# Two transformer-like blocks on one core: gate groups, projection and modulation moved; opening, border and end rewritten

## The chip, the cores and the metric

The kernel runs on one core of a Trainium2 chip. Five engines share the work: PE (TensorE, matrix products into PSUM banks), DVE (VectorE), ACT (ScalarE), POOL (GpSimd, nearly unused here) and SP (SyncE, which here only issues DMAs). Each engine takes its instructions in one fixed order. The metric is the time of one execution in microseconds of device time, lower is better.

## What is computed

The input has 512 tokens of width 2048. A first block (a gated convolution and a gated recurrence, their gated sum, and an embedding gate), a second block (dilated attention and two-way retention, modulated by a vector c) and a last norm follow one another. Cut to what matters:

```
def first_block(x, p, ...):
    h = rmsnorm(x, norm_mix_g)
    c_g, b_g, xa, za, q, fl, iv, og, ga, gb = split(h @ w_in)      # 4 x 1024, 4 x 1024, 2 x 2048
    ya = b_g * causal_dwconv3(c_g * xa, conv_w) * silu(za)
    o  = hgrn2_chunked(silu(q), kk(fl, lb), iv, log_f(fl, lb))     # 8 heads of 128
    yb = rmsnorm_per_head(o) * hg_norm_g * silu(og)
    m  = sigmoid(ga) * (ya @ w_a_out) + sigmoid(gb) * (yb @ w_b_out)
    x  = x + m @ w_o
    gate = sigmoid(rmsnorm(x, ple_norm_g) @ w_ple_gate)
    x  = x + gate * (p @ w_ple_proj)                               # p is 512 x 256
    return rmsnorm(x, final_norm_g)

def second_block(x, c, ...):
    shift, scale, gate = split(silu(c) @ w_ada + b_ada)            # w_ada is 2048 x 6144
    h = rms_norm(x, g) * (1 + scale) + shift
    q_a, k_a, v_a, z_a, q_r, k_r, v_r, z_r = split(h @ w_in)
    y = concat(dilated_attention_mixture(q_a, k_a, v_a) * silu(z_a),
               bidirectional_retention(q_r, k_r, v_r) * silu(z_r))
    x = x + gate * (y @ w_out)
    return rms_norm(x, final_gain)
```

## The kernel before, in words

**Products.** Activations stand in SBUF with features on partitions and the 512 tokens along the row, each as a rounded f32r part and a rest. Weights come from memory in chunks of 128x1024 f32 (512 KB). ACT makes the rounded part whi of a chunk (L245), DVE the rest wlo (L256). Each 128x128 weight tile then takes three matmuls of 128x512 (L355 to L357, in `mm3`): a chunk is 24 matmuls. Where the tokens are to be on partitions (`group_wide`), the three are L497 to L499. Ten gate groups go through a fast algorithm with 128x256 matmuls (L412 to L414). A group (`group_fm`) is 2 output tiles of 128 features: two PSUM banks of the pool ps_mm and 96 matmuls, when it has four chunks.

**PSUM.** There are eight banks: four of ps_mm for the large products, two of ps_sd and two of ps_so for side work. A product that needs a bank waits until the tile last in it has been read.

**What sets the order.** The program is written out by a Python planner: `chunk()` and `group_fm()` write the large products in a fixed plan (`plan_w`, `plan_wide`, `plan_dual`), and after each few matmuls call `tick()` (L156), which takes one step of a generator in each of the queues side, side2, post and slow. So the small work (norms, recurrence, modulation) is mixed into the products at those steps, and its place on DVE, ACT and PE is fixed when the program is written. `drain(cond)` (L171) takes steps until a condition holds.

**Stages in order**, with the time at which their first product starts in the trace: opening and norm of x with the first groups of w_in (0 us), the wide values w_v (57 us), the recurrence pairs pr = 1, 2, 3 with their groups fl, q and og (from 103 us), the plain gate groups i = 10 to 15 of w_in (up to 594 us), ten fast groups, w_a and w_b (1140 us), w_o (1314 us), w_gate (1488 us), the border to the second block with `dual("w_in2", ...)` (1664 us), w_v2 (1713 us), attention and retention, w_out (2375 us), whose last part is done in two halves of 256 tokens (from 2505 us), and the output.

**The places of the change.** `start_gen` (L702) squares the tokens' features, adds them (L715), makes row sums on PE (L574: the 128x128 squares are the weights and a column of ones the moving side), then sqrt (L720), reciprocal (L721), a diagonal matrix (L584) and a product with ones (L581, `spread`) that gives the norm factor R0 on all partitions (L726). Then it scales the features for later use (L739) and splits them (L545). The gate branch's first products are not yet normed and are scaled by R0 on the way out of PSUM (`times`, L984). `lower_bound` (L688) is a chain of small DVE instructions. `rec_gen` is the recurrence, whose last steps for pair 3 (exponentials L792 on ACT, products L895 and L898 on PE) run into the gate groups. `p_gen` and `ple_proj` (L1118) compute p @ w_ple_proj, one 128x1024 chunk for each of 4 groups: four ps_mm banks, 6 matmuls each, copied out by ACT (L1129) and DVE (L1131) and stored to memory. `ada_gen` (L1046) computes silu(c) @ w_ada row by row on DVE (L1068): each of 192 steps loads 256 KB. `h2_gen` (L1442) makes both norms at the border: two sums over partitions by products with ones (L561, L562, 128x512), a chain of 128x512 instructions and a reciprocal (L1457), then the features of the second block (L1466, L1467, L537, L543). `half_tail` and `finish` (L1849) close each half: row sums (L574), sqrt (L1854), reciprocal (L1855), diagonal (L584), spread (L581), a scaling of each of eight 128x512 pieces (L1864) and a DMA for each (L1865).

## Time and profile before

| what | value |
|---|---|
| time, median of 3 runs | 2569.77 us (2568.53 to 2569.97) |
| the profiled execution's own time | 2568.21 us |
| its span, first to last instruction | 2566.3 us |
| PE busy | 2535.8 us (99%) |
| DVE busy | 1724.2 us (67%) |
| ACT busy | 1023.8 us (40%) |
| mean granted TensorE clock | 0.994 of full speed |
| moved by DMA | 372 MB, mean 145 GB/s |

The span is what one execution's trace covers, and the time has some two microseconds more around it. PE is busy for nearly the whole span, so the table says only that the time is PE's work. A change that leaves the products alone can gain only what PE waits or runs slowly, and that is found place by place: in the windows (busy time and clock of a stretch), in the list of waits, and in the timeline of the stretch. A row of the trace such as "466.84 0.80 PE L355 ... [4.14 <-ACT s L1174]" reads: the instruction of line 355 started at 466.84 us and took 0.80 us, PE had stood idle for 4.14 us, and what ended the wait was ACT's instruction of line 1174. Matmuls overlap, so the distance of two starts, and not the duration, is what one costs.

### The profile page before, as it was taken

To read this page: it belongs to the slowest core of one execution; us is meant where nothing else is said; L and a number is where in the kernel's file an instruction comes from. 1 tells how busy PE (TensorE), PEld (TensorE's weight loads), DVE (VectorE), ACT (ScalarE), POOL (GpSimd) and SP (SyncE) were. 2 spreads that over 40 slices of the span, in tenths; PEclk is the share of its full clock that TensorE was granted. 3 is DMA by queue.
4 is the path that set the end of the run, shared out by engine and by line. 5 is a ranking of instruction groups with operands and counts; after the bars stand their busy time and mean duration, and the time that the engine had idled before them with its cause. 6 is when DMAs were issued, how large, how long until landed. Compare 5 with 4: busy or idle time off the path is not lost.

```text
span 2566.3 us, 34681 instructions
## 1 busy us (share of the span) xinstructions
PE 2535.8 (99%) x13796; PEld 2202.4 (86%) x13796; DVE 1724.2 (67%) x2938; ACT 1023.8 (40%) x1345; POOL 1.3 (0%) x9
## 2 busy tenths in 40 slices
PE   9999999899999999999999999999999999999998
PEld 7888888788999999998888888878888888888888
DVE  6768578787888988886656665576535446774445
ACT  6545255343344444443222344364323334442333
POOL 0000000000000000000000000000000000000000
PEclk9999999999999999999999999999999999999999
DMA  5322322474333334467656665352222325384345
GB/s 194 90 58 92 97 83 86 145 249 160 105 110 116 116 95 145 132 214 266 225 188 244 222 213 168 126 191 74 92 92 79 112 75 192 129 279 142 120 131 156
DMA packets 140595, 372.45 MB, mean 145 GB/s; under 512 B 15377, under 2 KB 20113, under 8 KB 140433
## 3 DMA queue, kind: packets, MB, share of 16 engines
q1 hardware_dynamic: 137680, 367.65, 43.9%
q10 hardware_dynamic: 2752, 2.58, 0.3%
q8 instruction: 108, 1.77, 0.3%
q14 instruction: 55, 0.44, 0.1%
HBM read 336.62 MB, written 33.55 MB: 144 GB/s over the span
## 4 chain that ended last, share of the span: by engine, by line
PE 95%; DMA 1%; ACT 1%; DVE 1%; issue 1%; ACTq 0%; DVEq 0%; SPq 0%
PE ps_mm L355 19%; PE ps_mm L357 19%; PE ps_mm L356 19%; PE ps_mm L414 3%; PE ps_mm L413 3%; PE ps_mm L412 3%; PE ps_mm L497 3%; PE ps_mm L499 3%; PE ps_mm L498 3%; PE ps_sd L414 2%; PE ps_sd L413 2%; PE ps_sd L412 2%; PE ps_so L414 1%; PE ps_so L413 1%; PE ps_so L412 1%; PE ps_sd L879 1%
## 5 line engine op out<-in xcount | busy, mean ns | idle before, releaser
L355 PE MATMUL ps_mm<-s,wlo 128*128 128x512 f32 (+1 forms) x2336 | 904.4, 387 | 7.1 <-ACT s L1174 4.8
L357 PE MATMUL ps_mm<-s,whi 128*128 128x512 f32 (+1 forms) x2336 | 898.3, 385 | 0.0
L356 PE MATMUL ps_mm<-s,whi 128*128 128x512 f32 (+1 forms) x2336 | 897.9, 384 | 0.0
L245 ACT ACTIVATE whi<-raw 128x1024 fp32r<-128x1024 f32 x338 | 357.3, 1058 | 755.7 <-PE ps_mm L357 486.8
L256 DVE TENSOR_TENSOR wlo<-raw,whi 128x1024 fp32r<-128x1024 f32 x338 | 412.5, 1221 | 365.3 <-ACT whi L245 361.0
L355 PEld LDWEIGHTS ps_mm<-s,wlo 128*128 128x128 f32 x2336 | 440.3, 188 | 95.0 <-ACT s L1174 5.9
L357 PEld LDWEIGHTS ps_mm<-s,whi 128*128 128x128 f32 x2336 | 440.3, 188 | 88.3
L356 PEld LDWEIGHTS ps_mm<-s,whi 128*128 128x128 f32 x2336 | 440.6, 189 | 85.3 <-DVE s L545 0.3
L268 ACT ACTIVATE whi<-raw 128x768 fp32r<-128x768 f32 x104 | 88.0, 846 | 281.9 <-issue 109.5
L497 PE MATMUL ps_mm<-whi,s 128*128 128x512 f32 x384 | 151.4, 394 | 6.2 <-DVE s L984 4.6
L499 PE MATMUL ps_mm<-whi,s 128*128 128x512 f32 x384 | 150.5, 392 | 0.0
L498 PE MATMUL ps_mm<-wlo,s 128*128 128x512 f32 x384 | 150.4, 392 | 0.0
L288 DVE TENSOR_TENSOR wlo<-raw,whi 128x768 fp32r<-128x768 f32 x104 | 99.5, 957 | 60.9 <-ACT whi L268 60.9
L293 DVE TENSOR_TENSOR s<-s,s 128x512 fp32r<-128x512 f32 x208 | 134.0, 686 | 5.9 <-ACT s L287 5.8
L1068 DVE SCALAR_TENSOR_TENSOR s<-s,s 128x512 f32<-128x512 f32 x184 | 123.7, 683 | 11.9 <-DMA s<-w_ada 11.8
L412 PE MATMUL ps_mm<-s,s 128*128 128x256 f32 x416 | 117.7, 283 | 0.0
L413 PE MATMUL ps_mm<-s,s 128*128 128x256 f32 x416 | 117.7, 283 | 0.0
L414 PE MATMUL ps_mm<-s,s 128*128 128x256 f32 x416 | 117.7, 283 | 0.0
L287 ACT ACTIVATE s<-s 128x1024 fp32r<-128x1024 f32 x104 | 108.9, 1047 | 14.5 <-DVE s L286 14.5
L537 ACT ACTIVATE s<-s 128x512 fp32r<-128x512 f32 x101 | 62.3, 628 | 77.0 <-DVE s L1682 50.1
L497 PEld LDWEIGHTS ps_mm<-whi,s 128*128 128x128 f32 x384 | 72.8, 189 | 21.9 <-issue 4.9
L413 PE MATMUL ps_mm<-s,whi 128*128 128x256 f32 x312 | 88.3, 283 | 0.0
(302 smaller groups left out, 3778.2 us busy)
## 6 DMA issues: line engine op xcount, KB each, us to landing
raw<-w_in SPq DMA_DIRECT2D x255, 512.0 KB, 3.7
s<-w_ada SPq DMA_DIRECT2D x192, 256.0 KB, 4.7
raw<-w_v SPq DMA_DIRECT2D x48, 512.0 KB, 3.5
raw<-w_out SPq DMA_DIRECT2D x40, 512.0 KB, 3.6
raw<-w_o SPq DMA_DIRECT2D x32, 512.0 KB, 4.6
raw<-w_gate SPq DMA_DIRECT2D x32, 512.0 KB, 4.4
s<-scr_x SPq DMA_DIRECT2D x48, 256.0 KB, 4.4
raw<-w_a SPq DMA_DIRECT2D x16, 512.0 KB, 3.8
```

Of the source, the lines that this page charges most:

```text
L245: S.activation(hi, r, AF.Copy)
L256: V.tensor_tensor(lo, r, f32(hi), op=ALU.subtract)
L293: V.tensor_tensor(tl[h], half(t, h), half(f32(th), h), op=ALU.subtract)
L355: PE.matmul(out, wlo[wsl], xhi[xsl], start=start, stop=False)
L356: PE.matmul(out, whi[wsl], xlo[xsl], start=False, stop=False)
L357: PE.matmul(out, whi[wsl], xhi[xsl], start=False, stop=stop)
L412: PE.matmul(R[r], wl, xh, start=k == 0 and r in (1, 2, 5, 3), stop=False)
L413: PE.matmul(R[r], wh, xl, start=False, stop=False)
L414: PE.matmul(R[r], wh, xh, start=False, stop=k == 7 and r in (6, 7, 4, 3))
L497: PE.matmul(banks[m], lo, whi[:, ws], start=kt == 0, stop=False)
L498: PE.matmul(banks[m], hi, wlo[:, ws], start=False, stop=False)
L499: PE.matmul(banks[m], hi, whi[:, ws], start=False, stop=kt == 15)
```

## The change

Six things are changed.

1. In the opening two more steps lie between the sum of squares and its row sums, and `lower_bound` comes two passes later in the loop that norms the features.
2. The og groups of the recurrence stand later in the plan, behind q of the next pair, and the last two at the end.
3. `ple_proj` leaves the gate groups i = 11 to 14 and stands behind the first four groups of w_o. Its banks are ps_sd and ps_so, no longer ps_mm.
4. The modulation's first 128 steps start with w_a and w_b (before, 40 steps ran in the gate groups, 40 in w_a and w_b, 48 in w_o). The consumer `gate_gen` waits for a flag.
5. At the border the sums over partitions become 128x1 row sums for all eight blocks of 128 tokens and two norms, small instructions, two diagonals and eight 128x128 spreads. The dual group reads its inputs by index as they come, and its first two banks are emptied (`leave2`) while its last chunk still runs.
6. The output tensor has two halves. The first is as before, all its DMAs on SP. The second is turned on PE: 32 transposes of 128x128 into eight PSUM banks, the norm factor then being a factor per partition in the copy out of PSUM (4 by ACT, 4 by DVE), with four DMAs of 512 KB. The diagonal, the spread and the eight scalings of this half are gone.

```diff
         gate_order = [g + z for g in range(8) for z in (0, 8)]
         plan_dual("w_in", 20, 16, 4)
-        for pr in range(4):
-            if pr > 0:
-                plan_w("w_in", [(20 + pr, 4)])
-            if pr % 2 == 0:
-                plan_wide("w_v", pr // 2)
-            if pr > 0:
-                plan_w("w_in", [(16 + pr, 4)])
-            plan_w("w_in", [(28 + pr, 4)])
+        plan_wide("w_v", 0)
+        plan_w("w_in", [(28, 4), (21, 4), (17, 4), (22, 4)])
+        plan_wide("w_v", 1)
+        plan_w("w_in", [(g, 4) for g in (18, 29, 23, 19, 30, 31)])
...
+        for g in range(8):
+            plan_w("w_o", [(g, 4)])
+            if g < 4:
+                plan_w("w_proj", [(g, 1)])
...
             A.free(pairs)
             yield
+            yield
+            yield
             b = ps_sd()
...
-                if k == 4:
+                if k == 6:
+                    lower_bound()
                     while not hold["x"]:
                         yield
-                    lower_bound()
-                    yield
...
+            for z in {1: (), 2: (1,), 3: (2, 3)}[pr]:
+                evac_og(cs[z], group_fm("w_in", 28 + z, h_act))
...
-                b = ps_mm()
+                b = ps("so" if m % 2 else "sd", 2)
...
-        slow.append(ada_gen(0, ADA[0]))
         for i in range(N_FAST, 16):
             g = gate_order[i]
-            if 0 <= i - PROJ_AT < 4:
-                ple_proj(i - PROJ_AT)
             if i == FORMS_AT:
...
+        slow.append(ada_gen(0, 128))
         for g in range(8):
-            if g == 1:
-                slow.append(ada_gen(ADA[0], ADA[1]))
+            if g == 6:
...
             post.append(residual_gen(g, xs))
+            if g < 4:
+                ple_proj(g)
...
-            s1, s2 = sums[0], sums[1]
-            b1 = yield from bcast_sum(s1)
-            b2 = yield from bcast_sum(s2)
-            ms = s1
-            V.tensor_scalar(ms, b1, 1.0 / D, EPS, op0=ALU.mult, op1=ALU.add)
-            V.tensor_scalar(rho, ms, EPS, None, op0=ALU.mult)
-            yield
-            V.scalar_tensor_tensor(out=rho, in0=b2, scalar=1.0 / D, in1=rho, op0=ALU.mult, op1=ALU.add)
-            S.activation(rho, rho, AF.Sqrt)
-            S.activation(R2, ms, AF.Sqrt)
-            V.reciprocal(rho, rho)
-            A.free(s2, ms)
+            b = ps_sd()
+            for t in range(8):
+                PE.matmul(b[:, t:t + 1], sums[t // 4][:, 128 * (t % 4):128 * (t % 4) + 128], f32(ones)[:, 0:1],
+                          start=True, stop=True)
+            ms, m2, both = small[:, 40:44], small[:, 44:48], small[:, 40:48]
+            V.tensor_scalar(ms, b[:, 0:4], 1.0 / D, EPS, op0=ALU.mult, op1=ALU.add)
+            V.tensor_scalar(small[:, 48:52], ms, EPS, None, op0=ALU.mult)
+            V.scalar_tensor_tensor(out=m2, in0=b[:, 4:8], scalar=1.0 / D, in1=small[:, 48:52],
+                                   op0=ALU.mult, op1=ALU.add)
+            S.activation(both, both, AF.Sqrt)
+            V.reciprocal(both, both)
+            diagonal(sums[1], m2, 4)
+            diagonal(sums[0], ms, 4)
+            yield
+            b1, b2 = ps_sd(), ps_sd()
+            spread(b2, sums[1], 4)
+            S.activation(rho, b2, AF.Copy)
+            hold["rho"] = True
+            spread(b1, sums[0], 4)
+            S.activation(R2, b1, AF.Copy)
+            A.free(sums[0], sums[1])
             yield
...
-        side.append(h2_gen())
-        b0, b1 = dual("w_in2", 0, 4, x2g_act)
+        post.append(h2_gen())
+        left2 = []
+
+        def leave2(banks):
+            drain(lambda: hold["rho"])
+            left2.extend(times(banks, rho))
+
+        b1 = dual("w_in2", 0, 4, x2g_act, wait_act(x2g_act), leave2)[1]
         A.free(*x2g_act)
         for _ in range(16):
-            if h2_act[0] is None:
+            if h2_act[1] is None:
                 tick()
-        b0, b1 = times(b0, rho), times(b1, rho)
+        b0, b1 = left2, times(b1, rho)
...
+            if (h, g) == (1, 7):
+                last.append(A.w())
+                for j in range(2):
+                    V.tensor_scalar(last[0][:, j, hs], x4[g][:, j, hs], vec("g_f2", 2 * g + j), None, op0=ALU.mult)
...
+        def finish_turned(sqs):
+
+
+            yield
+            b = ps_sd()
+            row_sums(b, [sums[3][:, H:T]], 2, last=False)
+            turned = {}
+
+            def turn(t, n, bank):
+                for i in range(4):
+                    c = H + 128 * t
+                    PE.transpose(bank[:, 128 * i:128 * i + 128], (x4[:7] + last)[2 * n + i // 2][:, i % 2, c:c + 128], ident)
+                turned[t, n] = bank
+
+            for t in range(2):
+                turn(t, 0, ps("so", 2))
+            row_sums(b, [sq[:, 0:H] for sq in sqs], 2, first=False)
+            r = R4[:, 2:4]
+            S.activation(r, b[:, 0:2], AF.Sqrt, bias=eps_t, scale=1.0 / D)
+            V.reciprocal(r, r)
+            for n in (1, 2):
+                for t in range(2):
+                    turn(t, n, ps_mm())
+            for t in range(2):
+                turn(t, 3, ps_sd())
+            rows = a["out"][1].rearrange("p a b -> (p a b)").rearrange("(t p d) -> p t d", t=2, d=D)
+            for n in range(4):
+                o = A.w()
+                S.activation(o[:, 0, :], turned[0, n], AF.Copy, scale=r[:, 0:1])
+                V.tensor_scalar(o[:, 1, :], turned[1, n], r[:, 1:2], None, op0=ALU.mult)
+                SY.dma_start(rows[:, :, 512 * n:512 * n + 512], o)
```

**Opening, DVE.** The rows are the copies out of PSUM of the first wide group (`times`, into s from ps_mm with R0; L984 before, L980 after), the weight rests wlo, and `lower_bound` (L691 to L699 before, L686 to L694 after). Before:

```order
L984 TENSOR_TENSOR s_500<-ps_mm_152,R_151 128x512
L984 TENSOR_TENSOR s_502<-ps_mm_153,R_151 128x512
L256 TENSOR_TENSOR wlo_484<-raw_406,whi_483 128x1024
L984 TENSOR_TENSOR s_517<-ps_mm_154,R_151 128x512
L984 TENSOR_TENSOR s_519<-ps_mm_155,R_151 128x512
L256 TENSOR_TENSOR wlo_526<-raw_456,whi_525 128x1024
L691 TENSOR_TENSOR tmp_92<-vecs 128x8
L693 COPY tmp_92<-tmp_92 128x8
L694 RECIPROCAL tmp_92<-tmp_92 128x8
L695 TENSOR_TENSOR tmp_92<-tmp_92 128x8
L696 TENSOR_TENSOR tmp_92<-tmp_92 128x8
L697 TENSOR_SCALAR tmp_92<-tmp_92 128x8
```

After:

```order
L254 TENSOR_TENSOR wlo_484<-raw_398,whi_483 128x1024
L686 TENSOR_TENSOR tmp_92<-vecs 128x8
L688 COPY tmp_92<-tmp_92 128x8
L689 RECIPROCAL tmp_92<-tmp_92 128x8
L690 TENSOR_TENSOR tmp_92<-tmp_92 128x8
L691 TENSOR_TENSOR tmp_92<-tmp_92 128x8
L692 TENSOR_SCALAR tmp_92<-tmp_92 128x8
L693 TENSOR_SCALAR onem<-tmp_92 128x8
L694 TENSOR_SCALAR floor<-tmp_92 128x8
L980 TENSOR_TENSOR s_534<-ps_mm_154,R_151 128x512
L980 TENSOR_TENSOR s_536<-ps_mm_155,R_151 128x512
```

The last two copies of the group (banks 154 and 155) stood ahead of the weight rest 526 and of `lower_bound`, and now stand behind all of it.

**Gate groups, PE.** The rows are the last products of the recurrence (L895, L898) and the second half of `ple_proj` for g = 0, which takes a new ps_mm bank for each 6 matmuls. Before:

```order
L895 MATMUL ps_so_3512<-s_3285,s_2277 128x128
L898 MATMUL ps_so_3512<-s_84,s_3325 128x64 x2
L355 MATMUL ps_mm_3532<-s_2729,wlo_3369 128x512
L356 MATMUL ps_mm_3532<-s_2729,whi_3368 128x512
L357 MATMUL ps_mm_3532<-s_2729,whi_3368 128x512
L355 MATMUL ps_mm_3532<-s_2732,wlo_3369 128x512
L356 MATMUL ps_mm_3532<-s_2732,whi_3368 128x512
L357 MATMUL ps_mm_3532<-s_2732,whi_3368 128x512
L355 MATMUL ps_mm_3541<-s_2729,wlo_3369 128x512
```

After, the same products are L891 and L894, and the group that follows is in the banks that it already had:

```order
L891 MATMUL ps_so_3685<-s_3088,s_2112 128x128
L894 MATMUL ps_so_3685<-s_3348,s_3531 128x64 x2
L353 MATMUL ps_mm_3512<-s_670,wlo_3573 128x512
L354 MATMUL ps_mm_3512<-s_670,whi_3572 128x512
L355 MATMUL ps_mm_3512<-s_670,whi_3572 128x512
L353 MATMUL ps_mm_3513<-s_670,wlo_3573 128x512
L354 MATMUL ps_mm_3513<-s_670,whi_3572 128x512
L355 MATMUL ps_mm_3513<-s_670,whi_3572 128x512
```

The projection has left this place, and the next four banks are taken over two groups.

**Border, DVE.** The rows are the second block's features (L1466 and L543 before, L1472 and L541 after), weight rests, and the four copies out of the dual group's banks (L984 before, L980 after) for which the first product of w_v2 waits. Before:

```order
L1466 TENSOR_TENSOR s_14943<-s_14943,R_151 128x512
L543 TENSOR_TENSOR s_14972<-s_14912,s_14972 128x512
L256 TENSOR_TENSOR wlo_14976<-raw_14861,whi_14975 128x1024
L256 TENSOR_TENSOR wlo_15018<-raw_14920,whi_15017 128x1024
L984 TENSOR_TENSOR s_14936<-ps_mm_14713,R_151 128x512
L984 TENSOR_TENSOR s_14943<-ps_mm_14714,R_151 128x512
L984 TENSOR_TENSOR s_15049<-ps_mm_14715,R_151 128x512
L984 TENSOR_TENSOR s_14963<-ps_mm_14716,R_151 128x512
L256 TENSOR_TENSOR wlo_15061<-raw_14978,whi_15060 128x1024
```

After:

```order
L541 TENSOR_TENSOR s_14953<-s_14894,s_14953 128x512
L1472 TENSOR_TENSOR s_14932<-s_14932,R_151 128x512
L541 TENSOR_TENSOR s_14959<-s_14901,s_14959 128x512
L254 TENSOR_TENSOR wlo_14963<-raw_14841,whi_14962 128x1024
L980 TENSOR_TENSOR s_14925<-ps_mm_14669,R_151 128x512
L980 TENSOR_TENSOR s_14932<-ps_mm_14670,R_151 128x512
L254 TENSOR_TENSOR wlo_15005<-raw_14909,whi_15004 128x1024
L980 TENSOR_TENSOR s_15036<-ps_mm_14671,R_151 128x512
L980 TENSOR_TENSOR s_14668<-ps_mm_14672,R_151 128x512
```

The copies of the first two banks stood behind two weight rests and all four in a row. Now they stand behind one, and the second rest follows them.

## Rows read from the trace of the kernel before

**Rows 1.** The page, part 4: the chain that ended last, by engine.
```profile
PE 95%; DMA 1%; ACT 1%; DVE 1%; issue 1%; ACTq 0%; DVEq 0%; SPq 0%
```

**Rows 2.** PE's waits: reader, releaser, us in total, times, the longest.
```profile
PE ps_mm L355 <- ACT s L1174: 4.8, 2, 4.1
PE ps_mm L497 <- DVE s L984: 4.6, 1, 4.6
PE ps_mm L355 <- DVE s L1131: 2.3, 2, 1.9
```

**Rows 3.** Windows: stretch, us; busy PE, PEld, DVE, ACT, POOL; clock, DMA share, GB/s.
```profile
0.00:30.00 30.00, 28.41 (x117) 23.06 (x118) 20.66 (x28) 22.61 (x33) 1.30 (x9) 1.00 0.82 297
30.00:60.00 30.00, 26.81 (x119) 21.99 (x118) 20.64 (x27) 13.02 (x18) 0.00 (x0) 0.94 0.31 101
...
455.00:485.00 30.00, 22.49 (x101) 17.55 (x99) 18.90 (x46) 13.08 (x20) 0.00 (x0) 0.83 0.45 147
...
1140.00:1314.00 174.00, 174.00 (x770) 144.08 (x769) 108.87 (x186) 50.04 (x61) 0.00 (x0) 1.00 0.71 237
1314.00:1488.00 174.00, 174.00 (x770) 144.06 (x769) 110.61 (x204) 53.16 (x66) 0.00 (x0) 1.00 0.68 233
...
1664.00:1715.00 51.00, 46.45 (x201) 38.10 (x200) 37.16 (x48) 30.76 (x42) 0.00 (x0) 0.97 0.63 214
```

**Rows 4.** Timeline of PE, 33 to 43 us: start, us, instruction, idle before.
```profile
33.42 0.39 PE L356 MATMUL ps_mm<-s,whi 128*128 128x512 f32 x1
33.65 0.39 PE L357 MATMUL ps_mm<-s,whi 128*128 128x512 f32 x1
37.23 1.05 PE L574 MATMUL ps_sd<-ones,s 128*128 128x1 f32 x8 [3.19 <-DVE s L715]
...
42.56 0.61 PE L581 MATMUL ps_sd<-s,ones 128*128 128x128 f32 x4
```

**Rows 5.** DVE by line, 43 to 82 us: count, busy us, mean ns, idle before.
```profile
L739 DVE TENSOR_TENSOR s<-s,R 128x512 f32<-128x512 f32 x14 | 9.4, 687 | 3.5 <-ACT R L726 3.5
L545 DVE SCALAR_TENSOR_TENSOR s<-s,vecs,s 128x512 fp32r<-128x512 f32 x12 | 9.0, 747 | 0.0
L256 DVE TENSOR_TENSOR wlo<-raw,whi 128x1024 fp32r<-128x1024 f32 x5 | 6.1, 1224 | 2.0 <-ACT whi L245 2.0
L984 DVE TENSOR_TENSOR s<-ps_mm,R 128x512 f32<-128x512 f32 x4 | 2.7, 692 | 3.1 <-PE ps_mm L357 3.1
```

**Rows 6.** Timeline of PE, 462 to 485 us.
```profile
475.72 0.66 PE L355 MATMUL ps_mm<-s,wlo 128*128 128x512 f32 x1 [1.88 <-DVE s L1131]
...
479.16 0.47 PE L357 MATMUL ps_mm<-s,whi 128*128 128x512 f32 x1
...
483.84 0.94 PE L838 MATMUL ps_so<-s,s 64*128 64x128 f32 x12 [1.48 <-ACT s L829]
```

**Rows 7.** Timeline of ACT, 455 to 476 us.
```profile
464.24 0.63 ACT L792 ACTIVATE s<-s 128x512 f32<-128x512 f32 x1 [2.62 <-DVE s L791]
```

**Rows 8.** Timeline of PE, 1700 to 1722 us.
```profile
1712.89 0.76 PE L497 MATMUL ps_mm<-whi,s 128*128 128x512 f32 x1 [4.55 <-DVE s L984]
...
1717.29 0.63 PE L498 MATMUL ps_mm<-wlo,s 128*128 128x512 f32 x1
1717.72 0.63 PE L499 MATMUL ps_mm<-whi,s 128*128 128x512 f32 x1
```

**Rows 9.** Timeline of DVE, 1695 to 1722 us.
```profile
1712.06 2.48 DVE L984 TENSOR_TENSOR s<-ps_mm,R 128x512 f32<-128x512 f32 x4
```

**Rows 10.** The chain that ended last, 2555 to 2567 us: start, us, what.
```profile
2555.60 0.18 DVE small L1855
...
2556.35 0.73 PE ps_sd L581 x4
...
2557.10 0.69 DVE s L1864
2557.79 0.59 DVEq L1954
```

**Rows 11.** DMA, 2553 to 2567 us, in 40 slices.
```profile
GB/s 339 336 340 354 342 351 193 23 26 6 0 0 0 0 0 0 184 319 363 334 340 342 351 334 354 316 363 342 339 328 360 334 357 313 21 0 0 0 0 0
```

**Rows 12.** Timeline of PE, 1778 to 1782 us.
```profile
1778.85 0.60 PE L1591 MATMUL ps_sd<-ident,s 128*128 128x128 f32 x4
1779.21 0.48 PE L355 MATMUL ps_mm<-s,wlo 128*128 128x512 f32 x1
```

57 lines of the change are left out of this document (25 added, 32 removed).

## The prediction

> **What bounds the kernel now.** I read the chain that ended last first: PE is 95% of it [rows 1], so the time is PE's products, and these do not change. What can change is PE's lost time, and three views tell where it lies: PE's waits by releaser [rows 2], the windows with busy time and granted clock [rows 3], and the timeline at each place. A loss has two parts. One is the wait itself. The other comes behind it: after a wait of some 4 us matmuls of 128x512 start 0.43 us apart [rows 8], where before the opening's wait they started 0.23 us apart [rows 4], because the granted clock has fallen to the lower of its two levels (1.2 GHz instead of 2.4) and PE has to work for some time before it rises. So idle time and clock are taken together, (length - busy) + (1 - clock) x length, from the windows of [rows 3]:
> - 30 to 60 us, the opening: 3.2 idle + 0.06 x 30 = 5.0 us.
> - 455 to 485 us, where the recurrence's tail meets the projection: 7.5 + 0.17 x 30 = 12.6 us.
> - 1664 to 1715 us, the border: 4.55 + 0.03 x 51 = 6.1 us, and 1.4 more behind the window, since seven matmuls from 1715 us on still start 0.43 apart [rows 8]: 7.5 us in all.
> Beside these there is the tail behind the last product. The change touches all four.
>
> **Gate groups, -13.7 us.** At 455 to 485 us PE waits twice for a ps_mm bank, 4.1 us for ACT's sigmoid copy L1174 and 1.9 us for the projection's copy L1131 [rows 2, 6]. The clock is low behind the first wait and again until 479.2 [rows 6]. The bank is late because ACT's copy stands in its queue behind an exponential of the recurrence, L792, which began only at 464.24 after waiting 2.62 us for DVE [rows 7]. The projection makes this matter: it asks for four banks in 24 matmuls (24 x 0.23 = 5.5 us), where a gate group asks for two in 96 matmuls (22 us). With the projection moved, the bank that ACT empties late is wanted a whole group later, so 22 us of products cover a lateness of some 4 us. All 12.6 us go, and with them the smaller pair of waits at the projection's fourth piece, (4.8 - 4.1) + (2.3 - 1.9) = 1.1 us [rows 2]. The moved modulation also leaves DVE here. Its 40 rows and the projection's 96 matmuls are not removed but moved, below.
>
> **New place of projection and modulation, 0.** The projection behind w_o groups 0 to 3 takes banks of ps_sd and ps_so, which no one else uses in that stage, and its next use is a w_o group later (27 us), so I expect no wait. The modulation adds 40 steps of 256 KB between 1140 and 1488 us (10.5 MB), the projection 2 MB of weights and 4 MB of stores. DMA there moved 237 x 174 + 233 x 174 = 81.8 MB [rows 3]. With 16.5 MB more over 348 + 22 us this is 266 GB/s. The opening ran at 297 GB/s at a DMA share of 0.82 [rows 3], so 266 should fit. DVE is busy 63% there [rows 3] and gains about 9 points, no bound.
>
> **Recurrence, +1.5 us.** With og groups moved, DVE has less cover where a pair's first score product (after: L872) follows the steps of the next pair. Counting instructions in the order against [rows 5] durations, DVE is done 1 to 2 us after PE arrives. The nearest row is a recurrence wait of 1.48 us at 483.84 [rows 6], which the reordering may also remove. I take 1.5, with 0 and 3.5 as ends.
>
> **Opening, -0.7 us.** The row sums waited 3.19 us for the sum of squares [rows 4]. Two more steps put 24 matmuls (5.5 us) ahead of them, so this wait and its slow stretch, 5.0 us, vanish. But the factor R0 depends on them: before, its product began at 42.56 [rows 4], and after it begins about 0.6 us later, since PE reaches the row sums at 39.5. From R0 on, DVE must do 16 scalings, 14 splits, 4 weight rests and 4 copies out of PSUM before the products at 80 us may run. By [rows 5] these are paced at about 0.61, 0.65, 1.14 and 0.68 us (durations less the overlap of neighbours), 26.1 us, with `lower_bound`, the gates' small steps and idle time 35 us, so to about 80.3 us. PE, now 5 us ahead, waits instead: in the order before the copies that stand behind `lower_bound`, and before two weight rests, about 1.1 + 2.4 + 2.5 us if nothing else gives. What remains of the gain is what DVE gains, 0.7 us. It is the least sure term. If DVE's idle time (3.5 + 2.0 + 3.1 us in [rows 5]) shrinks with earlier input, up to -3.5. If the clock falls behind the second and third wait, as it did behind a 1.88 us wait at 475.72 [rows 6], +2.5.
>
> **Border, -4.7 us.** PE waits 4.55 us there for copies out of PSUM (L984), which DVE does four in a row behind the features' work, until 1714.5 [rows 8, 9]. In the order after, two copies stand behind one weight rest while the dual's last chunk runs. Counting from the row sums, DVE reaches the first copy about 20 us later, the bank is full at 21, and w_v2 begins at 24, so about 2 us of slack: all 7.5 go. Added on PE: 8 row sums, four of which took 1.05 us [rows 4], so 1.9 with their overlap, and 8 spreads of two passes each; two spreads took 0.73 us [rows 10], of which the last pass's tail is hidden by what follows, so 1.6. Removed: 4 matmuls of 0.23. Between row sums and spread stand 12 matmuls (2.8 us), about as long as the small chain they cover, so 0.2 for a short wait. -7.5 + 3.5 - 0.9 + 0.2 = -4.7, with ends -6 and 0 (the copies as late as now, half the loss kept).
>
> **End, -2.0 us.** The reciprocal ends at 2555.78, then come diagonal, spread (0.73) and the first scaling, done at 2557.79 [rows 10]. After it, a scaling out of PSUM (0.69 by the nearest row, L984 [rows 5]) follows at once: first output at 2556.5, 1.3 us sooner. The remaining 2 MB go at 316 to 363 GB/s [rows 11], about 6.3 us. Larger pieces and the lack of waits for the next scaling give about 0.7 more. The 32 transposes cost PE 0.09 us each (four of L1591 move the next product by 0.36 us [rows 12]), eight of them ahead of the last row sums, while ACT still squares. Ends: -0.8 and -3.5.
> The Trainium skill, page "TensorE: Matmul & The Clock Gate", section Part 4 (PE-mode transpose), gives about 275 ns for a 128x128 transpose and says that they do not count as busy time for the clock. That would be 2.2 us for eight, more than one DMA of 512 KB needs. The trace has no such distance.
>
> **Sum.** -13.7 + 0 + 1.5 - 0.7 - 4.7 - 2.0 = -19.6 us. The profiled execution took 2568.2, so 2548.6 for such a run. The median of the runs shown is 1.6 above it: 2550.
>
> **Rivals.**
> A, the gate loss comes back elsewhere: its source, ACT behind DVE's recurrence steps, is untouched [rows 7], and PE may meet it at a ps_sd or ps_so bank of the recurrence. For it: 1.48 us at 483.84 is just such a wait [rows 6]. Against: 22 us of cover at ps_mm. Half of 13.7 stays: 2557. Chance 0.14.
> B, the opening and the recurrence give all they can, -3.5 instead of -0.7 and 0 instead of +1.5: 2550 - 4.3 = 2546. Chance 0.16.
> C, slower than before: DMA becomes the bound between 1140 and 1488 us. The stage needs 98.3 MB. PE needs 370 us for it. If loads mixed with stores and 256 KB rows sustain less than 252 GB/s, the stage takes over 390 us and the gain is gone. At 245 GB/s it takes 401 us, +31: 2581. Against: 297 GB/s with share 0.82 in the opening [rows 3]. Chance 0.03.
> D, the change does not do what it says at the border: the copies stay late, because the features' work on ACT and DVE fills the whole dual group. Then 7.5 us stay lost and 2.8 of new products come on top: 2550 + 7.5 = 2557.5. Against: the order. Chance 0.06.
> E, transposes run at a third of the pace of [rows 12], as after a fall of the clock: each DMA waits for eight transposes of 0.27 (2.2 us, against 1.55 for 512 KB at 340 GB/s), so 3 x 0.65 + 1.5 for the eight ahead of the row sums: +3.5, 2553.5. This is the skill's price, which [rows 12] speak against. Chance 0.06.
>
> **How the numbers follow.** The forecast's own case has 0.55: 2550, within 2547 and 2553.5. For 8 in 10 the range takes in B and the near ends of A and D: 2544 to 2557. A measurement of this kernel can tell about 0.2% (5 us) from no change, so faster means below 2564.6. All cases but C lie there, and for several mishaps at once I leave a little: faster 0.94, same 0.03, slower 0.03.
>
> **What would show it.** Right: the waits for L1174 and L1131 copies are gone, the window 455 to 485 us has a clock of 1.00, PE waits for DVE at about 55, 70 and 78 us for 1 to 2.5 us each, a recurrence wait of some 1.5 us lies between 300 and 400 us, w_v2 starts without a wait, and the first output DMA of the second half starts about 1.3 us earlier against the last product. Wrong: a clock below 1 in 60 to 90 us, waits of PE for weight rests or DMA in w_a to w_o, a wait at the first fast or gate group, or more than 12 us from the last product to the end of the span.

## The result

| kernel | median of runs, us | runs | ratio to before, with its 95% interval |
|---|---|---|---|
| before | 2569.81 | 4 (2568.53 to 2569.97) | 1 |
| changed | 2549.22 | 4 (2548.47 to 2550.19) | 0.9916 [0.9903, 0.9929] |

The change makes the kernel 20.6 us faster (0.8%); forecast were 2550 and a range of 2544 to 2557. The span of the profiled execution goes from 2566.3 to 2548.4 us, so 17.9 us can be followed in the two traces. (The profiled execution of the changed kernel was the slowest of its four, and that of the kernel before was faster than its median.) To see where they come from, take stage lengths between starts of products that both kernels have: the opening from the first product with a rounded weight to the first such product of the og group behind the first w_v, the gates from there to the first product of w_a (less 21.8 us, 96 matmuls, where the projection stands there), the border from the dual group's first product to the next w_in2 group behind w_v2, and the end from w_out's first product to the end of the span.

| stage, us | before | changed | difference | forecast |
|---|---|---|---|---|
| opening | 96.0 | 97.0 | +1.0 | -0.7 |
| gates with recurrence | 1015.7 | 1002.4 | -13.2 | -13.7 + 1.5 |
| w_a, w_b, w_o with the projection taken out | 348.2 | 348.2 | 0.0 | 0 |
| w_gate | 175.5 | 175.5 | 0.0 | 0 |
| border | 95.4 | 90.7 | -4.7 | -4.7 |
| attention, retention | 615.6 | 615.6 | 0.0 | 0 |
| end | 191.4 | 189.7 | -1.7 | -2.0 |

The differences are those of the unrounded lengths. The rest, 0.7 us, lies ahead of the first product. The 14 warm-up matmuls, which the change does not touch, took longer in this execution, and in the experiments below that start lies anywhere between 6.4 and 7.9 us.

PE's waits in the changed kernel of more than 0.2 us (reader, releaser, us in total, times, the longest):

```profile
PE ps_mm L496 <- DVE wlo L254: 4.3, 2, 2.3
PE ps_sd L661 <- DVE s L644: 1.6, 1, 1.6
PE ps_mm L495 <- DVE s L980: 0.7, 1, 0.7
PE ps_sd L872 <- DVE s L858: 0.5, 1, 0.5
```

The three rows of [rows 2] are gone: nothing waits for the gates' or the projection's copies, and the 4.6 us for the border's copy are gone too. New are the two waits for a weight rest, the one for L980 and the one of the recurrence (L872); that of L661 is the wait ahead of PE's first instruction, which both kernels have. The windows of the changed kernel, to be read like [rows 3]:

```profile
30.00:60.00 30.00, 29.27 (x137) 24.14 (x136) 25.91 (x41) 15.71 (x22) 0.00 (x0) 1.00 0.31 107
60.00:102.00 42.00, 37.70 (x158) 30.35 (x157) 25.37 (x36) 18.85 (x25) 0.00 (x0) 0.96 0.28 86
440.00:470.00 30.00, 30.00 (x166) 25.41 (x165) 22.98 (x48) 14.43 (x20) 0.00 (x0) 1.00 0.29 94
1650.00:1700.00 50.00, 50.00 (x238) 41.95 (x237) 33.16 (x48) 29.34 (x41) 0.00 (x0) 1.00 0.57 198
```

At the gates and at the border PE is busy all the time at the full clock. In the opening the loss has moved from 30 to 60 us into 60 to 102 us: 4.3 us idle and a clock of 0.96. The timeline of PE there:

```profile
72.99 0.50 PE L496 MATMUL ps_mm<-wlo,s 128*128 128x512 f32 x1 [2.05 <-DVE wlo L254]
...
80.98 0.50 PE L496 MATMUL ps_mm<-wlo,s 128*128 128x512 f32 x1 [2.26 <-DVE wlo L254]
...
82.27 0.63 PE L497 MATMUL ps_mm<-whi,s 128*128 128x512 f32 x1
82.70 0.63 PE L495 MATMUL ps_mm<-whi,s 128*128 128x512 f32 x1
...
85.21 0.40 PE L495 MATMUL ps_mm<-whi,s 128*128 128x512 f32 x1
```

Behind the second wait the matmuls start 0.43 us apart until 85.2, which is the lower clock level (1.2 GHz). At the border, PE's new row sums and spreads:

```profile
1673.92 1.84 PE L1446 MATMUL ps_sd<-ones,s 128*128 128x1 f32 x16
1678.48 1.95 PE L579 MATMUL ps_sd<-s,ones 128*128 128x128 f32 x16
```

Eight row sums and eight spreads (two passes each) take 1.8 and 1.9 us. Between their starts lie 4.56 us: 1.84 of row sums and 12 matmuls of 0.227, so PE never waits for the small chain. The end, all engines:

```profile
2538.93 1.94 PE L1897 MATMUL ps_mm<-ident,s 128*128 128x128 f32 x16
2539.10 0.26 ACT L1904 ACTIVATE small<-ps_sd,eps_t 128x2 f32<-128x2 f32 x1 [1.09 <-PE ps_sd L572]
2539.40 0.17 DVE L1905 RECIPROCAL small<-small 128x2 f32<-128x2 f32 x1 [1.32 <-ACT small L1904]
2539.60 0.69 ACT L1914 ACTIVATE s<-ps_so,small 128x512 f32<-128x512 f32 x1 [0.23 <-DVE small L1905]
...
2540.49 3.11 SPq L1916 DMA_DIRECT2D out<-s  x4
```

From the reciprocal's end (2539.57) to the first output DMA it is 0.9 us; in [rows 10] it was 2.0 us. Sixteen turns take 1.94 us, 0.12 at most each, and the granted clock holds (window of the changed kernel, columns as above):

```profile
2537.00:2542.00 5.00, 4.74 (x45) 4.51 (x43) 3.53 (x9) 3.47 (x7) 0.00 (x0) 1.00 0.31 114
```

### The profile page after: what moved, and what is told of

Its sections match the earlier page's. It is cut to its first block, busy times and chain, and to the rows that moved or that the text cites. A ratio compares the mean times of both kernels' runs of the same rounds, so it can differ in the third digit from the quotient of the medians.

```text
span 2548.4 us, 34697 instructions
## 1 busy us (share of the span) xinstructions
PE 2534.3 (99%) x13852; PEld 2203.9 (86%) x13852; DVE 1709.5 (67%) x2926; ACT 1016.9 (40%) x1336; POOL 1.3 (0%) x9
## 4 chain that ended last, share of the span: by engine, by line
PE 96%; DVE 2%; ACT 1%; issue 0%; DMA 0%; SPq 0%; DVEq 0%
PE ps_mm L353 19%; PE ps_mm L355 19%; PE ps_mm L354 19%; PE ps_mm L412 3%; PE ps_mm L411 3%; PE ps_mm L410 3%; PE ps_mm L495 3%; PE ps_mm L496 3%; PE ps_mm L497 3%; PE ps_sd L412 2%; PE ps_sd L410 2%; PE ps_sd L411 2%; PE ps_so L412 1%; PE ps_so L411 1%; PE ps_so L410 1%; PE ps_sd L875 1%
## 5 line engine op out<-in xcount | busy, mean ns | idle before, releaser
L353 PE MATMUL ps_mm<-s,wlo 128*128 128x512 f32 (+1 forms) x2304 | 889.0, 386 | 0.0
L355 PE MATMUL ps_mm<-s,whi 128*128 128x512 f32 (+1 forms) x2304 | 883.8, 384 | 0.0
L354 PE MATMUL ps_mm<-s,whi 128*128 128x512 f32 (+1 forms) x2304 | 883.0, 383 | 0.2 <-DVE s L543 0.2
L355 PEld LDWEIGHTS ps_mm<-s,whi 128*128 128x128 f32 x2304 | 432.9, 188 | 86.2
L354 PEld LDWEIGHTS ps_mm<-s,whi 128*128 128x128 f32 x2304 | 433.2, 188 | 84.7 <-DVE s L543 0.6
L353 PEld LDWEIGHTS ps_mm<-s,wlo 128*128 128x128 f32 x2304 | 433.1, 188 | 83.9
L1064 DVE SCALAR_TENSOR_TENSOR s<-s,s 128x512 f32<-128x512 f32 x176 | 118.6, 683 | 21.7 <-DMA s<-w_ada 21.7
L496 PEld LDWEIGHTS ps_mm<-wlo,s 128*128 128x128 f32 x384 | 72.4, 189 | 20.0 <-DVE wlo L254 5.1
```

The costliest lines, as they stand in the source:

```text
L353: PE.matmul(out, wlo[wsl], xhi[xsl], start=start, stop=False)
L354: PE.matmul(out, whi[wsl], xlo[xsl], start=False, stop=False)
L355: PE.matmul(out, whi[wsl], xhi[xsl], start=False, stop=stop)
L496: PE.matmul(banks[m], hi, wlo[:, ws], start=False, stop=False)
```

## Experiments

All medians are of four runs, each beside runs of the kernel before on the same chip (2569.5 to 2571.4 us). The kernel before itself differs by up to 1.9 us between sets of runs, so a small effect is read from the stage lengths of the traces, which agree to 0.1 us where PE waits for nothing. Each stage length is that of one execution. This is the table for all kernels (us):

| kernel | median | opening | gates | border | end |
|---|---|---|---|---|---|
| before | 2569.8 | 96.0 | 1015.7 | 95.4 | 191.4 |
| changed | 2549.2 | 97.0 | 1002.4 | 90.7 | 189.7 |
| e1: changed, opening of before | 2548.8 | 97.1 | 1002.4 | 90.7 | 189.8 |
| e2: changed, lower_bound ahead | 2547.7 | 94.8 | 1002.4 | 90.7 | 189.8 |
| e3: changed, projection back | 2547.7 | 94.9 | 1001.7 | 90.7 | 189.8 |
| e4: changed, modulation back | 2556.5 | 95.4 | 1010.5 | 90.7 | 189.8 |
| e5: before, modulation moved | 2555.3 | 97.8 | 1001.6 | 95.5 | 191.4 |
| e6: before, projection moved | 2558.4 | 97.4 | 1004.7 | 95.6 | 191.5 |
| e7: e4 with its silu in one step | 2554.1 | 95.7 | 1006.7 | 90.7 | 189.8 |
| e8: changed, no leave2 | 2549.1 | 95.6 | 1002.4 | 91.1 | 189.7 |
| e9: changed, old norm chain | 2552.9 | 94.9 | 1002.4 | 94.9 | 189.8 |
| e10: changed, old end | 2551.4 | 96.6 | 1002.4 | 90.7 | 191.9 |
| e11: e2 and e3 together | 2547.6 | 94.8 | 1001.7 | 90.7 | 189.8 |
| e12: e11 with two more DVE savings | 2543.3 | 91.1 | 1001.7 | 90.7 | 189.8 |

### The gates: projection or modulation?

e3 puts the projection back into gate groups 11 to 14, in ps_mm banks; the modulation stays moved.

```diff
+            if 0 <= i - 11 < 4:
+                ple_proj(i - 11)
...
-                b = ps("so" if m % 2 else "sd", 2)
+                b = ps_mm()
```

> The changed kernel with the projection put back into gate groups 11 to 14, with ps_mm banks as before; the modulation stays where the change put it. Theory: the projection's demand for four ps_mm banks in 24 matmuls behind the recurrence's tail is the cause of the 12.6 us, so most of it returns: +8 to +13, 2557 to 2562, with waits for the ACT and DVE copies of the projection at some 450 us and a clock below 0.9 in those 30 us. Rival 1: the modulation's DVE rows in the gates were the cause: then +0 to +3. Rival 2: the reordered og groups shifted the recurrence's tail away from this place, so that the projection finds free banks: +0 to +3 as well, and told from rival 1 by the next run.

Measured: 2547.7 us, gates 1001.7 us. Nothing of the loss returned; even the recurrence's wait (L872, 0.5 us) is gone. The prediction's cause falls for this arrangement. e4 does the reverse and puts the modulation's first 40 steps back.

```diff
+        slow.append(ada_gen(0, 40))
         for i in range(N_FAST, 16):
...
-        slow.append(ada_gen(0, 128))
+        slow.append(ada_gen(40, 128))
```

> The changed kernel with the modulation's first 40 steps put back into the gate groups; the projection stays behind w_o. Theory: DVE has room there and no bank is asked for in a hurry, so +0 to +1: 2549 to 2550. Rival 1 of the run before (DVE's modulation rows delay the recurrence's tail, which delays the banks): +6 to +12, with PE waits near 450 us.

Measured: 2556.5 us, gates 1010.5 us, 8.1 more than in the changed kernel. The first rival held in size. PE's wait, and ACT ahead of it (both timelines of e4):

```profile
463.42 2.07 PE L834 MATMUL ps_so<-s,s 64*128 64x128 f32 x14 [5.25 <-ACT s L825]
```
```profile
455.15 1.28 ACT L1050 ACT_TABLE_LOAD   x1
456.44 0.63 ACT L1050 ACTIVATE s<-s 128x512 f32<-128x512 f32 x1
456.98 1.05 ACT L243 ACTIVATE whi<-raw 128x1024 fp32r<-128x1024 f32 x1
458.05 1.28 ACT L788 ACT_TABLE_LOAD   x1
459.34 0.63 ACT L788 ACTIVATE s<-s 128x512 f32<-128x512 f32 x1
...
460.96 1.28 ACT L1050 ACT_TABLE_LOAD   x1
...
462.79 0.58 ACT L825 ACTIVATE s<-ps_sd 128x512 f32<-128x512 f32 x1
```

L1050 is the modulation's silu, L788 the recurrence's exponential. They alternate, and each turn loads another table: eight loads of 1.28 us between 444 and 465 us. The copy L825, which PE waits for, stands behind seven of them. No row of the modulation (L1064) has run on DVE by then, so it is not its rows that delay PE here, as the rival had it, but ACT's tables, and DVE's silu products, which wait up to 3.77 us for ACT. e7 takes most of the loads away by computing the four silu in one step; the modulation's rows stay in the gates.

```diff
                 A.free(sg)
-                yield
+            yield
```

> The changed kernel with the modulation's first 40 steps in the gates, as in the run before, but the four silu of its c_row computed in one step instead of four. In that run's trace ACT switched its table nine times from 444 to 463 us between the recurrence's exponentials and these silu, 1.28 us each. If the switches are what made PE wait 5.25 us, most of them go (two are left of eight), the wait falls below 1 us and the time to 2549 to 2551. If the DVE rows and their wait for w_ada's DMA make it, the wait stays above 3 us and the time above 2554.

Measured: 2554.1 us (runs from 2552.1 to 2557.9), gates 1006.7 us in the profiled one, which is the fastest. Between the two cases: six table loads fewer took away 3.8 of the 8.1 us by this pair of traces, 2.4 of 7.3 by the medians. The windows of e4 and e7 (columns as above) show that the larger part of it is clock (0.89 and 1.00), and that PE's idle time fell only from 5.25 to 3.91 us:

```profile
440.00:470.00 30.00, 24.75 (x119) 20.50 (x119) 19.90 (x42) 23.50 (x28) 0.00 (x0) 0.89 0.26 88
```
```profile
440.00:470.00 30.00, 26.09 (x140) 21.55 (x139) 24.27 (x55) 18.35 (x25) 0.00 (x0) 1.00 0.38 134
```

The waits that stay, on DVE and on PE (timeline of DVE, then PE's waits in e7):

```profile
455.03 0.69 DVE L1064 SCALAR_TENSOR_TENSOR s<-s,s 128x512 f32<-128x512 f32 x1 [3.22 <-DMA s<-w_ada]
```
```profile
PE ps_so L834 <- ACT s L825: 2.4, 1, 2.4
...
PE ps_mm L353 <- DVE wlo L254: 1.5, 1, 1.5
```

DVE stands still for 3.22 us because the modulation's first row waits for its DMA; a weight rest and the recurrence's steps queue behind it. Against the changed kernel, counted from the same product, DVE's steps from that weight rest on are 7.8 us late: 3.9 by the four silu products and a wait of 1.35 us for ACT ahead of them, the rest by the load and its row. So putting the modulation back costs in two ways, through ACT's tables and silu products, and through a DVE queue held by a load.

These runs have the og groups moved. Which of the two mattered in the kernel before was asked with one edit each on that kernel. e5 moves the modulation alone, e6 the projection alone.

```diff
-        slow.append(ada_gen(0, ADA[0]))
...
+        slow.append(ada_gen(0, 128))
         for g in range(8):
-            if g == 1:
-                slow.append(ada_gen(ADA[0], ADA[1]))
```

> The kernel before with one edit: the modulation's first 128 steps moved to w_a and w_b as in the change; the projection and the og groups stay in the gates. New theory, after the runs with one of them put back (projection back: no loss; modulation back: +7): the modulation's DVE rows and ACT table switches in the gates delay the recurrence's tail, and the projection's hurry for banks only decides where PE meets that. Then this edit alone removes nearly all of the 12.6 us and the smaller pair: 2556 to 2559, with a clock near 1 from 455 to 485 us. Rival (the prediction's theory, that the projection's demand for four banks makes the loss as soon as the recurrence's tail and the groups stand as they did before): 2566 to 2570, with waits for the projection's copies.

```diff
-            if 0 <= i - PROJ_AT < 4:
-                ple_proj(i - PROJ_AT)
...
+            if g < 4:
+                ple_proj(g)
```

> The kernel before with one edit: the projection moved behind w_o groups 0 to 3, in ps_sd and ps_so; modulation and og groups stay. New theory: the recurrence's tail is still late, so PE waits at another place of it, for a ps_so or ps_sd product, and half or more of the loss stays: 2561 to 2567. Rival (prediction): the 12.6 and 1.1 us go: 2556 to 2558.

Measured: e5 2555.3 us, gates 1001.6, so all 14.1 us of that stage gone with the modulation alone. e6 2558.4 us, gates 1004.7: 11.0 gone with the projection alone, 3.1 left. Neither theory held in full. The late exponential in e5, to set against [rows 7], and PE's wait in e6:

```profile
462.15 0.63 ACT L792 ACTIVATE s<-s 128x512 f32<-128x512 f32 x1 [2.00 <-DVE s L791]
```
```profile
475.95 1.16 PE L839 MATMUL ps_so<-s,s 64*128 64x128 f32 x14 [2.37 <-ACT s L830]
```

Counted from the projection's first product (457.6 us before, 460.4 in e5), that exponential starts 6.6 us later in the kernel before and 1.7 us later in e5. The 4.9 us between them come from DVE, whose row held the modulation's work there too. Counted in the same way, the two timelines of DVE agree to 0.1 us until 435.6 us. Then, in the kernel before, the modulation's first silu product waits for ACT, which loads the silu's table first (timeline of DVE, kernel before):

```profile
437.54 0.69 DVE L1055 TENSOR_TENSOR s<-s,s 128x512 f32<-128x512 f32 x1 [1.62 <-ACT s L1054]
```

This wait and product put DVE 2.3 us back, the three silu products behind it 1.4 more, and two rows of the modulation 1.2: together the 4.9 us. The load that the first of these rows waits for costs nothing, although it looks the longest: where DVE waits 2.23 us for w_ada in the kernel before, it waits 2.31 us for PE at the same place in e5 (timelines of DVE, kernel before, then e5):

```profile
455.72 0.69 DVE L1068 SCALAR_TENSOR_TENSOR s<-s,s 128x512 f32<-128x512 f32 x1 [2.23 <-DMA s<-w_ada]
```
```profile
454.86 0.69 DVE L862 TENSOR_TENSOR s<-ps_sd,s 128x512 f32<-128x512 f32 x1 [2.31 <-PE ps_sd L879]
```

That explains PE's first wait (4.1 us for L1174). The second (1.9 us for L1131) has another cause, which the trace of the kernel before shows on ACT and DVE. First the second sigmoid copy, then the projection's first two copies (timelines of ACT and DVE, kernel before):

```profile
468.92 0.60 ACT L1174 ACTIVATE s<-ps_mm 128x512 f32<-128x512 f32 x1 [2.12 <-DMA scr_sga<-s]
...
472.23 0.60 ACT L1129 ACTIVATE s<-ps_mm 128x512 f32<-128x512 f32 x1 [1.78 <-DMA scr_sga<-s]
```
```profile
474.98 0.69 DVE L1131 COPY s<-ps_mm 128x512 f32<-128x512 f32 x1 [3.26 <-DMA scr_pp<-s]
```

Each of these copies waits until the store of the copy before it has landed, as if the pool of SBUF buffers had only one left for them. In e5 the two sigmoid copies follow each other at once (timeline of ACT, e5), and neither in e5 nor in e6 does any copy of this stage wait for a store:

```profile
464.10 1.09 ACT L1175 ACTIVATE s<-ps_mm 128x512 f32<-128x512 f32 x2
```

So the loss of 12.6 us needed both parts. The modulation made the recurrence's tail some 5 us late, and with both in the gates the copies waited for each other's stores, which gave the second wait and the slow stretch behind it. That both together emptied the pool is argued from these waits and from the buffers that the two hold; no run varied the pool. Without the projection PE meets the lateness at the recurrence's own product and loses 3 us; without the modulation neither the lateness nor the waits for stores are there.

No run puts the og groups back alone. With them as before, e5 has the same gates (1001.6 us) as e3 has with them moved (1001.7), so none of the gain is seen to hang on them.

### The opening

e1 restores the opening of before; e2 moves lower_bound's DVE chain ahead, into the time in which DVE waits for R0.

```diff
-            yield
-            yield
             b = ps_sd()
...
-                if k == 6:
+                if k == 4:
```

> The changed kernel with the opening of before: row sums two steps earlier, lower_bound in the loop's pass 4. My theory: the opening is bound by DVE from the norm factor R0 on, so the change there only moves PE's loss from 34 us (one wait of 3.2 us and a slow stretch) to three waits at 55, 70 and 78 us. Then this kernel shows the wait for L574's row sums again (3.2 us, 2 us of slow matmuls behind it), no waits at 70 and 78 us, and by the traces is about 0.6 us faster: 2548.6, between 2547 and 2550. Rival 1: the change of the opening gains what I forecast (0.7) or more: 2550 to 2553. Rival 2: all of the 1.7 us by which the changed kernel's trace stands later at its first recurrence group (104.52 against 102.78 us) belongs to the opening: 2547.5. What tells them apart first is the start of the 409th product, counted from the first.

```diff
+            bound = lower_bound()
+            next(bound)
             yield
...
             row_sums(b, [acc], 4)
+            next(bound, None)
...
                 if k == 6:
-                    lower_bound()
```

> The changed kernel with lower_bound's small DVE chain moved ahead: its first two instructions behind the sum of squares, the rest behind the row sums, where DVE waits for R0 (1.5 us idle before the reciprocal, 1.9 us before the first scaling). Theory (DVE-bound from R0 on): the 1.9 us between the weight rest of 53.3 us and the copies of 56.1 us leave DVE's path, the wait at 55.7 us goes (0.7), the waits at 70 and 78 us shrink by up to 1.9 together with the 1.5 us slow stretch behind the last: 2 to 3.5 us faster than the changed kernel, 2546 to 2547. Rival: DVE's later idle (2.06 us at 61 us for ACT's sigmoids, whose table load was hidden by nothing) absorbs it: the waits at 70 and 78 us stay and only 0.7 is gained, 2548.5.

Measured: e1 2548.8 us, opening 97.1 with the row-sum wait (2.4 us) and its slow stretch back, no waits at 70 and 78 us. So old and new opening are equal in this pair of traces. But the same new opening took 97.0, 94.9, 95.4, 95.7, 95.6, 94.9 and 96.6 us in the changed kernel, e3, e4, e7, e8, e9 and e10, and the old one 96.0, 97.1, 97.8 and 97.4 us in the kernel before, e1, e5 and e6. By the middle of each the change gains 1 to 2 us; with a spread of 2 us within each it is not settled better than that. The spread has a cause that can be seen, the clock. In e3 the wait at 78 us is as long as in the changed kernel, but no slow stretch follows (timeline of PE, e3):

```profile
80.75 0.50 PE L496 MATMUL ps_mm<-wlo,s 128*128 128x512 f32 x1 [2.26 <-DVE wlo L254]
81.09 0.40 PE L497 MATMUL ps_mm<-whi,s 128*128 128x512 f32 x1
81.33 0.40 PE L495 MATMUL ps_mm<-whi,s 128*128 128x512 f32 x1
```

In e4, e7 and e8 the slow stretch follows the wait at 70 us instead; PE then comes later to the next weight rest and waits 0.6 us for it and not 2.3.

e2: 2547.7 us, opening 94.8, 2.3 less than in the changed kernel by the traces, 1.5 by the medians, where the DVE-bound theory had 2 to 3.5. The wait at 56 us is gone and the one at 70 us fell from 2.05 to 1.45 us, while the one at 78 us kept 2.2 us and the slow stretch stayed. PE's idle time there falls from 5.0 to 3.7 us; what the trace gains beyond these 1.4 us lies within the spread.

### The border

e8 leaves out leave2: all four copies stand behind the dual group. e9 keeps leave2 and restores the norm chain of before.

```diff
-        b1 = dual("w_in2", 0, 4, x2g_act, wait_act(x2g_act), leave2)[1]
+        b0, b1 = dual("w_in2", 0, 4, x2g_act, wait_act(x2g_act))
...
-        b0, b1 = left2, times(b1, rho)
+        b0, b1 = times(b0, rho), times(b1, rho)
```

> The changed kernel without leave2: all four copies out of the dual group's banks stand behind its end, the norm chain by row sums stays. Theory of the prediction: the copies' place is what decides; but the shorter norm chain has brought the features' work forward, so that DVE reaches the copies about when the group ends: the wait returns with 1 to 2 us of the 4.55, without a fall of the clock: 2550 to 2551. Rival 1: leave2 is the whole gain, the wait is 4 us and the slow stretch is back: 2555 to 2557. Rival 2: the norm chain is the whole gain: 2549, no wait above 0.8 us.

```diff
+            b1 = yield from bcast_sum(s1)
+            b2 = yield from bcast_sum(s2)
...
-            spread(b2, sums[1], 4)
-            S.activation(rho, b2, AF.Copy)
+            V.reciprocal(rho, rho)
+            hold["rho"] = True
```

> The changed kernel with the border's norm chain of before (sums by 128x512 products with ones, 128x512 sqrt and reciprocal), but with leave2 kept. The run without leave2 lost only 0.3 us at the border, so the new chain is what pays. Theory: with the old chain PE waits there again, 1 us or more even with leave2, and the border is 2 to 7 us longer from the dual group's first product to the second w_in2 group: 2551 to 2556. Rival: either of the two is enough alone (leave2 lets the planner put the copies ahead of the features): no wait, and the old chain, which has fewer products on PE (0.9 instead of 3.5 us), is 2 to 3 us faster: 2546 to 2547.

Measured: e8 2549.1 us, border 91.1, 0.4 more than the changed kernel, as its second rival had it. e9 2552.9 us, border 94.9, 4.2 more, as its theory had it. The copies on DVE in e8, and PE's wait and DVE's reciprocal in e9:

```profile
1695.90 1.23 DVE L254 TENSOR_TENSOR wlo<-raw,whi 128x1024 fp32r<-128x1024 f32 x1 [2.46 <-ACT whi L243]
1697.04 2.48 DVE L980 TENSOR_TENSOR s<-ps_mm,R 128x512 f32<-128x512 f32 x4
```
```profile
PE ps_mm L495 <- DVE s L980: 4.6, 2, 3.8
```
```profile
1686.78 3.36 DVE L1454 RECIPROCAL R<-R 128x512 f32<-128x512 f32 x1 [1.89 <-ACT R L1452]
```

In e8 the four copies stand in a row as before, but begin at 1697.0, while the dual's last matmul starts at 1697.4. In e9 the two early copies exist, and PE waits 3.8 us for them, since the features' scalings, which stand ahead of them on DVE, cannot begin before the 128x512 reciprocal has ended at 1690.1. It is the short chain that brings the features' work, and with it the copies, forward; where the copies stand hardly matters.

### The end

e10 restores the end of before.

```diff
-            (side, side2)[h].append((finish, finish_turned)[h](sqs))
+            (side, side2)[h].append(finish(h, sqs))
```

> The changed kernel with the end of before (diagonal, spread, eight scalings, eight DMAs for the second half, on two queues). By the two traces from the first product of w_out the end takes 1.6 us less in the changed kernel, so 2550.8 here, within 2549.5 and 2552.5. The row to look at: from the last 128x256 product to the last DMA's landing. Rival: the gain is the run's own spread, then within 0.5 us of the changed kernel in that stretch.

Measured: 2551.4 us, end 191.9, 2.1 us more than with turned outputs. Some 0.5 of it is clock: in e10 the granted clock was 0.50 from 2539.6 to 2540.9 us, where PE waits 0.6 and 1.1 us, and the spread took 1.22 us, where it took 0.73 in the kernel before [rows 10]. The DMA rates over the tail, in 40 slices, e10 (2536 to 2552 us), then the changed kernel (2535 to 2549 us):

```profile
GB/s 346 269 253 340 346 343 33 0 0 0 0 0 0 0 0 0 236 335 320 369 325 353 330 348 328 364 333 346 343 338 351 225 0 0 0 0 0 0 0 0
```
```profile
GB/s 360 340 339 304 348 336 354 342 144 0 0 0 0 0 0 0 0 0 298 386 351 392 375 392 357 380 398 328 421 374 381 374 386 363 35 0 0 0 0 0
```

Both tails are full of transfer: against the kernel before, the gain is an earlier start (1.1 us from the reciprocal) and a higher rate, about 375 GB/s with four transfers of 512 KB from one queue against 340 with eight of 256 KB from two. The rows in memory are also longer (2 KB against 1 KB); which of these makes the rate was not tested.

### Two versions from the findings

e11 joins e2 and e3. e12 adds a dummy sigmoid that loads ACT's table early, and gives the first pair's two scalings by 1 - lb to ACT.

> A version from the findings: the changed kernel with lower_bound moved ahead (2.3 us by the trace of that run against the changed kernel at the first recurrence group) and the projection back in the gate groups (no loss, 0.5 us less at the recurrence). Theory: the two add: 2546 to 2547, 2 to 3 us faster than the changed kernel. Rival: the projection's hurry for banks meets another place of the recurrence because everything comes 2 us earlier: 2550 and more, with waits near 455 us.

```diff
+                    S.activation(tmp8[:, 0, :], tmp8[:, 0, :], AF.Sigmoid)
...
+                if pr == 0:
+                    S.activation(KK[:, j, :], KK[:, j, :], AF.Copy, scale=onem[:, hd:hd + 1])
```

> The version before with two more DVE savings between 45 and 80 us: a dummy sigmoid of 128x8 loads ACT's table before the first pair's sigmoids (DVE idles 2.06 us there, 1.28 of them for the table), and the first pair's two scalings by 1 - lb (0.5 us each) go to ACT. Theory (DVE-bound until 80 us): 2.2 us less before the weight rest that PE waits for at 69 us, so that wait goes and the next one keeps 1.5 us: 1.5 to 2.2 us faster than the version before: 2544 to 2545. Rival: ACT, which now has 1.2 us more between 60 and 66 us, delays the rounded parts that DVE waits for: 0 to 0.5.

Measured: e11 2547.6 us (ratio to before 0.9914 [0.9897, 0.9930]), with opening 94.8 and gates 1001.7, so the stages keep what each edit gave. e12 2543.3 us (0.9899 [0.9884, 0.9914]), opening 91.1: 3.7 us less than e11 where 1.5 to 2.2 were expected. PE's waits in e12, all of them:

```profile
PE ps_mm L496 <- DVE wlo L254: 1.7, 1, 1.7
PE ps_sd L661 <- DVE s L644: 1.6, 1, 1.6
```

The wait at 69 us went as expected, the one at 74 us kept 1.7, and no slow stretch follows it, which was not in the expectation: of the 3.7 us 2.0 are waits and the rest is clock. Whether the edit keeps the clock up or chance did is not shown. e12 is the fastest version measured.

## Why the prediction was right, and where it was not

**What bounds the kernel.** Right. PE's lost time by stage was the thing to add up, and the sum of the parts that the trace resolves, +1.0 - 13.2 - 4.7 - 1.7 + 0.7, is the 17.9 us of the spans. The forecast 2550 is 0.8 us off the median. That is in part luck: for the profiled execution the sum gave 2548.6 and it took 2550.2, with the gates 1.0 us better than forecast and the opening 1.7 worse.

**Gates.** The size was right (-13.2 against -12.2 with the recurrence's term), the cause half right. The prediction named the projection's need for four banks in 5.5 us and treated the late exponential as given; its rival A even said that this source is "untouched". It is not: e5 shows that the modulation on DVE and ACT made it late, and that moving the modulation alone takes the whole loss away. The step that failed is the reading of [rows 7]: the wait of 2.62 us for DVE was read as the recurrence's own pace, and DVE's timeline further back, where the modulation's silu products and rows stand among the recurrence's steps and the first of them waits 1.62 us for ACT, was not followed. In the same way the wait for L1131 [rows 2] was put down to the demand for banks, where that copy itself waited 3.26 us for a store. Rival A's mechanism exists, as e4 shows (5.25 us at a ps_so product), but only while the modulation is in the gates.

**Recurrence.** The wait at L872 is there, 0.47 us at 385.0 instead of 1.5 us.

**New place.** Right: w_a to w_gate took the same time to 0.1 us, at 257 GB/s between 1110 and 1480 us, above the 252 that rival C put in doubt.

**Opening.** The mechanism was right: DVE binds from R0 on, PE waits from 56.1, 70.9 and 78.7 us on (0.7, 2.05 and 2.26 us against 1.1, 2.4 and 2.5), and e2 and e12 gain by freeing DVE. The term of -0.7 lies within what the traces show, between about +1 and -2, because the clock falls behind one of the waits in some executions and not in others; the prediction had this as the end of its range, not as chance from run to run. A clock below 1 between 60 and 90 us was one of its own signs of being wrong, and the trace has it (0.96).

**Border.** The size was right to 0.1 us, the cause wrong. The 7.5 us were credited to the two early copies; e8 shows these to be worth 0.4 us, and with the old chain they are worth some 0.5 (95.4 in the kernel before, 94.9 in e9). The short chain, which the prediction priced only as added products, is worth 4.2 of the 4.7 us net. The step that failed is that the old copies' lateness was put down to their place in DVE's row, while the reciprocal of 3.36 us and the wait of 1.89 us for ACT's sqrt ahead of it set when that row began. The 0.2 us for a short wait did not occur, and the spreads took 1.9 instead of 1.6 us.

**End.** -1.7 of -2.0 by this pair of traces, -2.1 by e10 with its 0.5 of clock. The first transfer starts 1.1 instead of 1.3 us sooner, and the rate gives the rest. Rival E fell: a turn costs at most 0.12 us. The Trainium skill, page "TensorE: Matmul & The Clock Gate", section Part 4 (PE-mode transpose), has some 275 ns for one of 128x128 in bf16 and says that it does not count as PE being busy in the same way for the clock. The first agrees with the trace as the duration of one (0.27 us, here in f32) and not as what one costs: 16 in a row take 1.94 us. On the second the traces do not agree: the granted clock of that stretch is 1.00, and in the ten traces with the turned end it falls 8 to 10 us behind the start of the last product, in the four without turns 3 to 5 us behind it.

Two of the errors, at gates and border, left the total untouched, because the change moved both candidate causes at once. A right sum over a stage says little about which edit earned it.

## What to carry to other kernels

Where an engine waits, follow the releaser's own queue back until something waits for nothing on chip: here ACT waited for DVE, and DVE was late by an unrelated background task in its queue, whose first step had in turn waited for ACT's table. A long wait in that queue need not be the cause: compare with the kernel without it, where another wait may stand at the same place (2.23 us for a load, 2.31 us for PE). Small work that alternates with other work on ACT can pay a table load each time (eight of 1.28 us in e4), and a load not yet landed holds what is queued behind its reader (3.22 us of DVE in e7). Copies that wait for a store (2 to 3 us each here) point at the buffers that a background task holds. When two moved parts could each explain a gain, put each back alone, on the new kernel and on the old.

## What the runs showed of the hardware

A wait of the same length, 2.26 us at the same place, was followed by a fall of the granted clock in the changed kernel (matmuls 0.43 us apart for 3.4 us, 1.7 us lost by the clock of 0.96 over 42 us) and by none in e3. The opening, one instruction stream in both, therefore spreads by about 2 us (97.0 and 94.9), which is as much as the smaller edits here are worth. And output transfers of 512 KB in rows of 2 KB ran at about 375 GB/s where 256 KB in rows of 1 KB ran at 340.
